# New prices and a shared read resource in the planner that orders a kernel's instructions

## The chip, the core and the metric

The kernel runs on one core of a Trainium2 chip. Five queues run side by side on it: TensorE (PE, whose weight loads are shown as PEld), VectorE (DVE), ScalarE (ACT), GpSimd (POOL) and SyncE (SP, which issues DMAs). Each takes its instructions strictly in the order in which the program holds them; between queues semaphores make an instruction wait for what it needs. The metric is the device time of one execution in microseconds (us), lower is better.

## The reference

One layer of a hybrid encoder over 2048 tokens of 1024 channels. All is float32.

```python
hn = rmsnorm(h, mix_norm_g[i])
proj = hn @ w_in[i]
u, g_ssm, q, k, v, g_attn = jnp.split(proj, SPLITS, axis=-1)
y_ssm = s5_branch(u, ...)                      
y_ssm = y_ssm * jax.nn.silu(g_ssm)
y_att = stick_breaking_branch(q, k, v, q_norm_g[i], k_norm_g[i]) * jax.nn.silu(g_attn)
h = h + jnp.concatenate([y_ssm, y_att], axis=-1) @ w_out[i]
ple_gate = jax.nn.sigmoid(rmsnorm(h, ple_norm_g[i]) @ w_ple_gate[i])
h = h + ple_gate * (p[i] @ w_ple_proj[i])
```

The state-space branch has 32 groups of 16 channels with a 64-wide complex state; each step needs a recurrence over the sequence. The attention branch has 8 heads of 64. For a block of 128 queries it computes, with z the scaled scores, weights exp(log_sigmoid(z) + the sum of log_sigmoid(-z) over all later keys before the query), strictly causal. In the kernel that sum of logarithms is a running product.

## The kernel before

**Stages.** First the input is normalised and transposed, and u is projected (`phase_u`). Then eight batches of four state-space groups run (`ssm_pack`, `ssm_batch`), with the gates of that branch (`gate_unit`) and the first attention projections among them. Attention follows: four head pairs, each over 16 query blocks, skewed by eight blocks against one another; while it runs, the projections of later blocks (`attn_proj`) and the GLU of the state-space branch (`glu_z`, `glu_unit`) are placed among it. Last come the output projection and the per-layer gate for 16 blocks of 128 tokens (`phase_out`). Products in float32 are made from three matmuls of values that are split into a high and a low part (`mm3`, L542 to L544, and `mm3x`, L657 to L659); the split takes one ACT copy (L514 or L492) and one DVE subtraction (L60 or L71).

**State space.** `ssm_pack` makes the matrices of a batch: on DVE the products bn and tm (L60, 128x1024), on POOL the three products at L350 to L352 (stC and tm, 128x1024); PE transposes bn (L358), ACT copies it into stB (L359). `ssm_batch` multiplies (ps_b, L407), rotates on DVE and POOL (rot at L60, swp at L419), scans (L421), goes through a chain of short DVE instructions on 32 columns (b_en, b_ew, the scan b_h at L439, b_H) with swaps of partition halves on ACT (L428, L429), scans again (L450), rotates back (L453 on POOL), and yields. Later PE makes ps_y from it (L467 to L470).

**Attention.** A block of `attn_block` takes its keys in pieces of up to 512. For a piece and each of two heads: PE scores (ps_z, L718, row-tiled), ACT two sigmoids (px at L723, be at L728), POOL a causal mask on the diagonal (two selects, L732), DVE the running product (`tensor_tensor_scan`, L734, which reads px twice), POOL the multiply be by px (L736). Then PE transposes be in 64x64 tiles (ps_wt, L527), ACT or DVE copies it (ws, L745 or L743), and PE multiplies by the values (ps_o, L753, column-tiled). A projection adds 24 matmuls of 512 columns (ps_qk), a root mean square whose power runs on POOL (L508, 128x4), a normalisation on DVE (qn), and transposes (ps_tq). So DVE and POOL both work on data in SBUF during the same microseconds.

**The order.** The program is written in a natural order; `arrange` then fixes the order of every queue. `plan` walks over all instructions, finds what each one must wait for, and prices it with `duration`, which gives two numbers: how long the engine is taken, and how much later the result is there. `list_schedule` plays the program by these prices: the engine that is free first takes the ready instruction of the lowest rank; a change of PE between row-tiled, column-tiled and full matmuls costs 0.2 us and is avoided within 4 us of rank; DMAs share a link. `best_order` plays it forward and backward six times, taking the times of each pass as ranks of the next, and keeps the forward order with the earliest planned end. Only that order reaches the chip: neither a planned time nor a planned wait does. On the chip an instruction starts as soon as it heads its queue and its inputs are there. The lines below are those of before; the change lies behind them, so that L numbers of the stages are the same in both kernels.

Of the kernel before, what the change touches and what calls it, by code (L numbers as in the profile page):

```python
# [1048 lines left out]
def duration(i, name, outs, ins, psum):  # L1049

    n = max([a[1] for a in outs + ins] or [1])
    eng = str(i.engine).split(".")[-1]
    if name == "InstDMACopy":
        return (0.6 if eng == "Pool" else 0.45), 0.0
    if name == "InstMatmult":
        cols, kind = outs[0][1], ins[0][2]
        if i.is_transpose:
            return (0.031 if ins[0][0] <= 64 else 0.109), 0.12
        if "float32r" in kind or "bfloat16" in kind:
            return {512: 0.228, 256: 0.120}.get(cols, max(cols / 2255.0, 0.058)) / (2 if ins[0][0] <= 64 else 1), 0.12  # L1060
        half = min(outs[0][0], ins[0][0]) <= 64
        return (1 if half else 2) * max(cols / 1160.0, 0.056), 0.12
    if eng == "Activation":
        return 0.193 + n * 0.00082, 0.0
    if eng == "Pool":
        if name == "InstTensorTensor" and "pow" in str(i.op).lower():
            return 0.45 + 0.15 * n, 0.0
        base, slope = {"InstMemset": (0.1, 0.0008), "InstTensorCopy": (0.5, 0.001), "InstTensorScalarPtr": (0.3, 0.001), "InstTensorScalarAffineSelect": (0.35, 0.0008)}.get(name, (0.47, 0.00175))
        return base + slope * n, 0.0
    if name == "InstTensorScalarPtr" and i.is_tensor_tensor_scan:  # L1070
        return 0.22 + n * 0.0027, 0.0
    if name in ("InstMemset", "InstTensorCopy") and not psum:
        return 0.11 + n * 0.0006, 0.0
    return 0.15 + n * 0.00107, 0.0


def plan(tc, pools):

    mybir_i = list(tc.nc.cur_bb.bb.instructions)
    first, last = 16512, 229344  # L1080
    open_l, open_r, base, slots, spans, over, home, used = [], [], {}, {}, [], {}, {}, {}
    for p in sorted(pools, key=lambda p: p.id):
        kb = int(p.kb_per_partition_size() * 1024)
        if str(p.space).split(".")[-1] != "SB":
            base[p.id] = 0
        else:
            side = open_r if "right" in str(p.side) else open_l
            born = int(p.alloc_inst.name.split("-")[1])
            while side and side[-1][2] is not None and side[-1][2] < born:
                side.pop()  # L1090
            at = side[-1][0] if side else (last if side is open_r else first)
            lo = at - kb if side is open_r else at
            end = p.release_inst
            side.append((lo if side is open_r else lo + kb, p.id, None if end is None else int(end.name.split("-")[1])))
            base[p.id] = lo
            for q, l2, h2, e2 in spans:
                if l2 < lo + kb and lo < h2 and e2 is not None and int(e2.name.split("-")[1]) < int(p.alloc_inst.name.split("-")[1]):
                    over.setdefault(p.alloc_inst.name, []).append(e2.name)
            spans.append((p.id, lo, lo + kb, end))
        for sp, size, tag, addr, _ in p.gen_slots(0):  # L1100
            home[tag] = p.alloc_inst.name, p.release_inst.name if p.release_inst is not None else None
            slots.setdefault(tag, []).append((str(sp).split(".")[-1], base[p.id] + addr, size // P))
    turn, tiles, held, pre, length, opened, soft, mode = {}, {}, {}, [], [], {}, [], {}
    number = {i.name: k for k, i in enumerate(mybir_i)}
    for k, i in enumerate(mybir_i):
        if type(i).__name__ == "BassTilePoolBoundary":
            pre.append(set())
            soft.append({number[q] for q in over.get(i.name, [])} | used.get(i.name, set()))
            length.append((0.0, 0.0, 0))
            continue  # L1110
        need, ins, outs, loose, psum = set(), [], [], set(), False
        for w, accs in ((0, i.ins), (1, i.outs)):
            for a in accs:
                b = getattr(a, "bass_ap", None)
                if b is None:
                    continue
                t, n = b.tensor, 1
                ap = [(int(s), int(c)) for s, c in b.ap]
                for s, c in a.ap[1:]:
                    n *= int(c)  # L1120
                (outs if w else ins).append((int(a.ap[0][1]), n, str(a.dtype)))
                if type(t).__name__ != "Tile":
                    continue
                shape = tuple(int(x) for x in t.shape)
                if t.name not in tiles:
                    mine = slots[t.tag]
                    q = turn[t.tag] = turn.get(t.tag, -1) + 1
                    sp, lo, size = mine[-q % len(mine)]
                    tiles[t.name] = rec = (sp, [], [], k)
                    if t.tag in opened:  # L1130
                        loose.add(opened[t.tag])
                    opened[t.tag] = k
                    if sp != "DRAM":
                        kept = []
                        for l2, h2, r2 in held.get(sp, []):
                            if l2 < lo + size and lo < h2:
                                need.update(r2[2])
                                if lo <= l2 and h2 <= lo + size:
                                    continue
                            kept.append((l2, h2, r2))  # L1140
                        held[sp] = kept + [(lo, lo + size, rec)]
                sp, accesses, users, born = tiles[t.name]
                loose.add(born)
                a0, r0 = home[t.tag]
                loose.add(number[a0])
                used.setdefault(r0, set()).add(k)
                if sp == "PSUM":
                    psum = True
                    f = (0, P, 1)
                    w = 1  # L1150
                elif sp == "DRAM":
                    row = shape[-1] if len(shape) < 3 else shape[1] * shape[2]
                    o = int(b.offset)
                    reach = o + sum((c - 1) * s for s, c in ap if s > 0)
                    f = (o // row, reach // row + 1, -1)
                else:
                    f = seen_footprint(tuple(ap), int(b.offset), shape)
                kept = []
                for r in accesses:
                    j, wj, g = r  # L1160
                    if j != k and (w or wj) and f[0] < g[1] and g[0] < f[1] and f[2] & g[2]:
                        need.add(j)
                        if w and f[0] <= g[0] and g[1] <= f[1] and (f[2] == -1 or (g[2] != -1 and not g[2] & ~f[2])) and sp != "DRAM":
                            continue
                    kept.append(r)
                accesses[:] = kept + [(k, w, f)]
                users.append(k)
        need.discard(k)
        loose.discard(k)
        pre.append(need)  # L1170
        soft.append(loose - need)
        length.append(duration(i, type(i).__name__, outs, ins, psum) + ((outs[0][0] * outs[0][1] * 4 if type(i).__name__ == "InstDMACopy" else 0),))
        if type(i).__name__ == "InstMatmult":
            mode[k] = "rows" if ins[0][0] <= 64 else "cols" if outs[0][0] <= 64 else "all"
    return mybir_i, pre, soft, length, mode


_seen = {}
# [9 lines left out]
def list_schedule(ops, pre, soft, length, mode, rank, near=4.0, change=0.2):  # L1188

    import heapq  # L1190
    n = len(ops)
    eng = [f"none{k}" if type(i).__name__ == "BassTilePoolBoundary" else str(i.engine) for k, i in enumerate(ops)]
    after, open_, free, wait, ready, order, now = [[] for _ in ops], [len(p) + len(q) for p, q in zip(pre, soft)], {}, {}, {}, {}, {}
    start, done, link = [0.0] * n, [0.0] * n, 0.0
    for k in range(n):
        for q in (*pre[k], *soft[k]):
# [16 lines left out]
    for _ in range(n):  # L1213
        best = None
        for e in free:
            while wait[e] and wait[e][0][0] <= free[e]:
                _, r, k = heapq.heappop(wait[e])
# [9 lines left out]
        t, late, e = best  # L1227
        if late:
            k = heapq.heappop(wait[e])[2]
        else:  # L1230
            m = min((h for h in ready[e] if ready[e][h]), key=lambda h: ready[e][h][0][0] - near * (h == now[e]))
            k = heapq.heappop(ready[e][m])[1]
        t = max(t, due(k))
        if now[e] != mode.get(k):
            t += change
            now[e] = mode.get(k)
        start[k] = t
        free[e] = t + length[k][0]
        if length[k][2]:
# [89 lines left out]
```

## Time and profile before

| | us |
|---|---|
| runs, three | 1605.84, 1606.33, 1608.09 |
| median | 1606.33 |
| span of the profiled execution, from its first to its last instruction | 1604.8 |
| mean granted TensorE clock over the span | 0.986 |
| instructions | 31108 |

The profiled execution has no time of its own but its span. A group of the profile reads: line, engine, operation, tile written <- tiles read, shapes, count | busy time in us, mean ns of one | idle time of the engine before them and who ended it. A row of waits reads: who waited <- for whom: us in total, times, longest. A row of the timeline reads: start, duration, engine, line, operation, tiles. The row of a stretch gives for each engine its busy time and, in brackets, its instructions, then the clock that the TensorE throttle granted (1 is full), the share of the DMA engines and GB/s. A matmul's duration holds its way through the array, so that neighbours overlap.

### The profile page before, as it was taken

How to read it: one execution, taken by the hardware profiler on the slowest of the kernel's cores; microseconds unless marked ns; L12 is line 12 of the kernel's file. 1: busy time of each engine (PE TensorE's matmuls, PEld its weight loads, DVE VectorE, ACT ScalarE, POOL GpSimd, SP SyncE). 2: the span in 40 equal slices, each digit the busy share in tenths (PEclk: the TensorE clock that was granted, in tenths of full speed). 3: DMA queues.
4: the chain of work that ended last, by engine and by line, in shares of the span. 5: the costliest groups of instructions: out<-in, count | busy, mean ns of one | idle time of the engine just before them, and what ended most of it. 6: DMA issues, size and time to landing. Idle time of an engine off the chain costs nothing.

```text
span 1604.8 us, 31108 instructions
## 1 busy us (share of the span) xinstructions
PE 1548.5 (96%) x11878; PEld 1254.5 (78%) x11878; DVE 1079.1 (67%) x1980; ACT 825.2 (51%) x1850; POOL 766.3 (48%) x882
## 2 busy tenths in 40 slices
PE   6999898999999999999999999999989999999998
PEld 6998888987777777777777776777678788888887
DVE  6895948868678997789987899748764432332322
ACT  6643435456566776677766777646544221121211
POOL 2242434437578898688967798747630000000000
PEclk9999999999999999999999999999999999999999
DMA  9897535455332323323233234432354221212210
GB/s 294 262 289 194 175 118 181 156 174 193 113 113 84 112 91 132 113 85 108 95 132 112 86 109 112 109 96 68 107 164 126 83 79 50 86 60 69 64 49 33
DMA packets 147670, 195.58 MB, mean 122 GB/s; under 512 B 63697, under 2 KB 110753, under 8 KB 136129
## 3 DMA queue, kind: packets, MB, share of 16 engines
q1 hardware_dynamic: 145552, 186.45, 36.1%
q0 software_dynamic: 1968, 7.15, 2.2%
q8 instruction: 94, 1.54, 0.4%
q14 instruction: 56, 0.45, 0.1%
HBM read 145.44 MB, written 48.12 MB: 121 GB/s over the span
## 4 chain that ended last, share of the span: by engine, by line
PE 79%; DVE 11%; issue 4%; POOL 3%; ACT 1%; DMA 1%; SPq 0%; POOLq 0%; DVEq 0%; ACTq 0%
PE ps_qk L657 7%; PE ps_qk L659 7%; PE ps_qk L658 7%; PE ps_o L753 6%; PE ps_z L718 5%; PE ps_wt L527 4%; PE ps_g L659 4%; PE ps_h L657 4%; PE ps_h L658 4%; PE ps_g L658 4%; PE ps_h L659 4%; PE ps_g L657 4%; DVE px L734 3%; POOL be L736 2%; PE ps_u L543 2%
## 5 line engine op out<-in xcount | busy, mean ns | idle before, releaser
L736 POOL TENSOR_TENSOR be<-be,px 128x512 f32<-128x512 f32 (+3 forms) x320 | 404.1, 1275 | 136.6 <-DVE px L734 51.0
L734 DVE TENSOR_TENSOR_SCAN px<-px 128x512 f32<-128x512 f32 (+3 forms) x320 | 424.6, 1338 | 52.6 <-ACT px L723 37.0
L723 ACT ACTIVATE px<-ps_z 128x512 f32<-128x512 f32 (+3 forms) x320 | 170.0, 539 | 78.8 <-PE ps_z L718 51.9
L657 PE MATMUL ps_qk<-w_w,xt 128*128 128x512 f32 x480 | 198.7, 414 | 1.2 <-DVE gn L60 1.2
L658 PE MATMUL ps_qk<-w_w,xt 128*128 128x512 f32 x480 | 195.4, 407 | 0.0
L659 PE MATMUL ps_qk<-w_w,xt 128*128 128x512 f32 x480 | 195.3, 407 | 0.0
L508 POOL TENSOR_TENSOR rs_h<-rs_h,mhalf 128x1 f32<-128x1 f32 x16 | 9.1, 572 | 381.8 <-DVE rs_h L67 381.8
L728 ACT ACTIVATE be<-ps_z 128x512 f32<-128x512 f32 (+3 forms) x320 | 170.4, 545 | 5.4 <-PE ps_wt L527 5.4
L745 ACT ACTIVATE ws<-ps_wt 128x512 f32<-128x512 f32 (+3 forms) x256 | 129.0, 540 | 79.3 <-PE ps_wt L527 78.5
L718 PE MATMUL ps_z<-k,q 64*128 64x512 f32 (+3 forms) x960 | 138.5, 392 | 2.4 <-ACT be L728 1.5
L753 PE MATMUL ps_o<-ws,v 128*64 128x128 f32 x2176 | 138.3, 278 | 0.0
L753 PEld LDWEIGHTS ps_o<-ws,v 128*64 128x64 f32 x2176 | 118.7, 138 | 22.2 <-issue 18.1
L527 PEld LDWEIGHTS ps_wt<-ident,be 64*128 64x128 f32 x2176 | 83.1, 138 | 51.6 <-issue 25.6
L657 PEld LDWEIGHTS ps_qk<-w_w,xt 128*128 128x128 f32 x480 | 90.2, 188 | 32.1 <-issue 11.9
L659 PEld LDWEIGHTS ps_qk<-w_w,xt 128*128 128x128 f32 x480 | 90.3, 188 | 24.2 <-issue 5.7
L658 PEld LDWEIGHTS ps_qk<-w_w,xt 128*128 128x128 f32 x480 | 90.5, 189 | 23.5 <-issue 5.8
L527 PE MATMUL ps_wt<-ident,be 64*128 64x64 f32 x2176 | 102.9, 229 | 5.8 <-POOL be L736 2.8
L514 ACT ACTIVATE yr<-yt 128x512 fp32r<-128x512 f32 x32 | 20.2, 632 | 162.7 <-PE ps_h L659 157.3
L657 PE MATMUL ps_h<-w_w,yr 128*128 128x512 f32 x256 | 100.7, 393 | 2.3 <-ACT yr L514 2.3
L659 PE MATMUL ps_g<-w_wg,hr 128*128 128x512 f32 x256 | 101.5, 397 | 0.0
L658 PE MATMUL ps_g<-w_wg,hr 128*128 128x512 f32 x256 | 101.1, 395 | 0.0
L658 PE MATMUL ps_h<-w_w,yr 128*128 128x512 f32 x256 | 100.6, 393 | 0.0
(378 smaller groups left out, 3608.5 us busy)
## 6 DMA issues: line engine op xcount, KB each, us to landing
xt<-hn SPq DMA_DIRECT2D x60, 1024.0 KB, 4.9
hn<-xt SPq DMA_DIRECT2D x16, 1024.0 KB, 9.5
wst<-in_w_in_dram SPq DMA_DIRECT2D x48, 256.0 KB, 5.3
xg<-hn SPq DMA_DIRECT2D x12, 1024.0 KB, 7.0
x<-in_x_dram SPq DMA_DIRECT2D x16, 512.0 KB, 7.0
out_dram<-o SPq DMA_DIRECT2D x32, 256.0 KB, 2.0
h<-in_x_dram SPq DMA_DIRECT2D x15, 512.0 KB, 4.3
u<-uq POOLq DMA_DIRECT2D x4, 1024.0 KB, 18.3
```

The costliest lines, as they stand in the source:

```text
L527: e.nc.tensor.transpose(ps[h][:, 64 * k:64 * k + 64], v[r], e.ident[r, r])
L543: mm(out, wh, xl, start=False, stop=False)
L657: mm(out, xh, wh, start=first, stop=False)
L658: mm(out, xh, wl, start=False, stop=False)
L659: mm(out, xl, wh, start=False, stop=last)
L718: nc.tensor.matmul(z[:, :n], q[half[h], a], A.k[ch][half[h], b, :n], start=s == 0, stop=s == 2)
L723: nc.scalar.activation(px[:, :n], z[:, :n], AF.Sigmoid, scale=-(HD ** -0.5))
L728: nc.scalar.activation(be[:, :n], z[:, :n], AF.Sigmoid, scale=HD ** -0.5)
L734: nc.vector.tensor_tensor_scan(rv, rv, rv, initial=1.0 if carry[h] is None else carry[h], op0=ALU.mult, op1=ALU.bypass)
L736: nc.gpsimd.tensor_tensor(be[:, :n], be[:, :n], px[:, 1:n + 1], op=ALU.mult)
L745: nc.scalar.activation(dst, ps, AF.Copy)
L753: nc.tensor.matmul(po[half[h], :P], A.v[sb][:, h], w[:, h, b], start=sb == i, stop=sb == 0)
```

## The change

All of it is in the planner. `duration` gets other numbers: most engine times are shorter, and most instructions get a delay of 0.03 to 0.11 us between the end of the engine time and the result, where it was 0 before (0.12 on PE). `plan` counts for each instruction the tiles in SBUF that it reads with more than one element to a partition, and `shares` marks instructions from that: on POOL any that reads one, on DVE any that reads two, and a copy or an operation with a scalar that reads one and touches no PSUM. In `list_schedule` marked instructions of the two engines exclude each other: `port` holds the time at which the last marked one ends, and the next starts no earlier.

```diff
@@ duration
         if i.is_transpose:
-            return (0.031 if ins[0][0] <= 64 else 0.109), 0.12
+            return (0.031 if ins[0][0] <= 64 else 0.109), 0.11
         if "float32r" in kind or "bfloat16" in kind:
-            return {512: 0.228, 256: 0.120}.get(cols, max(cols / 2255.0, 0.058)) / (2 if ins[0][0] <= 64 else 1), 0.12
+            return max(cols / 2400.0 + 0.0136, 0.107) / (2 if ins[0][0] <= 64 else 1), 0.11
...
     if eng == "Activation":
-        return 0.193 + n * 0.00082, 0.0
+        return (0.05 if psum else 0.094) + n * 0.00083, 0.065 if psum else 0.03
     if eng == "Pool":
         if name == "InstTensorTensor" and "pow" in str(i.op).lower():
-            return 0.45 + 0.15 * n, 0.0
-        base, slope = {"InstMemset": (0.1, 0.0008), "InstTensorCopy": (0.5, 0.001), "InstTensorScalarPtr": (0.3, 0.001), "InstTensorScalarAffineSelect": (0.35, 0.0008)}.get(name, (0.47, 0.00175))
-        return base + slope * n, 0.0
+            return 0.35 + 0.15 * n, 0.08
+        base, slope = {"InstMemset": (0.04, 0.0008), "InstTensorCopy": (0.4, 0.001), "InstTensorScalarPtr": (0.25, 0.001), "InstTensorScalarAffineSelect": (0.14, 0.0008)}.get(name, (0.12, 0.00186))
+        return base + slope * n, 0.09
     if name == "InstTensorScalarPtr" and i.is_tensor_tensor_scan:
-        return 0.22 + n * 0.0027, 0.0
-    if name in ("InstMemset", "InstTensorCopy") and not psum:
-        return 0.11 + n * 0.0006, 0.0
-    return 0.15 + n * 0.00107, 0.0
+        return 0.05 + n * 0.0022, 0.03
+    if name in ("InstMemset", "InstTensorCopy", "InstTensorScalarPtr") and not psum and not i_tt(i):
+        return 0.07 + n * 0.0006, 0.03
+    return 0.07 + n * 0.00104, 0.03
+
+def i_tt(i):
+    return getattr(i, "is_scalar_tensor_tensor", False)
@@ plan
+                read += not w and n > 1 and type(t).__name__ == "Tile" and slots_space(slots, t.tag) == "SB"
...
-        length.append(duration(...) + ((... DMA bytes or 0),))
+        length.append(duration(...) + ((... DMA bytes or 0), shares(i, type(i).__name__, read, psum)))
+
+def slots_space(slots, tag):
+    return slots[tag][0][0]
+
+def shares(i, name, read, psum):
+    eng = str(i.engine).split(".")[-1]
+    if eng == "Pool":
+        return read > 0 and name != "InstDMACopy"
+    return eng == "DVE" and (read > 1 or (read == 1 and not psum and name in ("InstTensorCopy", "InstTensorScalarPtr")))
@@ list_schedule
-    ..., now = ..., {}
+    ..., now, port = ..., {}, 0.0
...
         if now[e] != mode.get(k):
             t += change
             now[e] = mode.get(k)
+        if length[k][3]:
+            t = max(t, port)
+            port = t + length[k][0]
         start[k] = t
         free[e] = t + length[k][0]
```

Shapes, tiles, buffers, matmuls, DMAs and their number are those of before.

More of the change, by code (lines that the diff above doesn't have):

```diff
@@ L1108, in plan @@
             soft.append({number[q] for q in over.get(i.name, [])} | used.get(i.name, set()))
-            length.append((0.0, 0.0, 0))
+            length.append((0.0, 0.0, 0, False))
             continue
-        need, ins, outs, loose, psum = set(), [], [], set(), False
+        need, ins, outs, loose, psum, read = set(), [], [], set(), False, 0
         for w, accs in ((0, i.ins), (1, i.outs)):
@@ L1171, in plan @@
         soft.append(loose - need)
-        length.append(duration(i, type(i).__name__, outs, ins, psum) + ((outs[0][0] * outs[0][1] * 4 if type(i).__name__ == "InstDMACopy" else 0),))
+        length.append(duration(i, type(i).__name__, outs, ins, psum) + ((outs[0][0] * outs[0][1] * 4 if type(i).__name__ == "InstDMACopy" else 0), shares(i, type(i).__name__, read, psum)))
         if type(i).__name__ == "InstMatmult":
@@ L1192, in list_schedule @@
     eng = [f"none{k}" if type(i).__name__ == "BassTilePoolBoundary" else str(i.engine) for k, i in enumerate(ops)]
-    after, open_, free, wait, ready, order, now = [[] for _ in ops], [len(p) + len(q) for p, q in zip(pre, soft)], {}, {}, {}, {}, {}
+    after, open_, free, wait, ready, order, now, port = [[] for _ in ops], [len(p) + len(q) for p, q in zip(pre, soft)], {}, {}, {}, {}, {}, 0.0
     start, done, link = [0.0] * n, [0.0] * n, 0.0
```

## The prediction

> **What bounds the kernel now.** The change alters no instruction, only the order in which each engine's queue holds them, so the first question is what an order can win. I read the page's busy shares and its chain of waits.
>
> ```profile
> PE 1548.5 (96%) x11878; PEld 1254.5 (78%) x11878; DVE 1079.1 (67%) x1980; ACT 825.2 (51%) x1850; POOL 766.3 (48%) x882
> PE 79%; DVE 11%; issue 4%; POOL 3%; ACT 1%; DMA 1%; SPq 0%; POOLq 0%; DVEq 0%; ACTq 0%
> ```
>
> PE is busy for 1548.5 of 1604.8 us, and the chain that ends last runs through PE for 79% and through DVE for 11%. An order can win back at most the 56 us in which PE idles, the time it loses at a lower clock, and what it spends on changing the kind of matmul. Next, the stretches: projection of u and state-space part (0 to 330), attention (330 to 1185), output (1185 on). Columns: PE, weight loads, DVE, ACT, POOL busy, clock, DMA.
>
> ```profile
> 0.00:330.00 330.00, 297.19 (x2428) 287.10 (x2429) 248.76 (x599) 163.84 (x337) 116.82 (x81) 0.95 0.67 206
> 330.00:1185.00 855.00, 838.01 (x7412) 631.94 (x7411) 688.09 (x1154) 568.45 (x1351) 640.34 (x785) 0.99 0.35 113
> 1185.00:1605.00 420.00, 413.26 (x2042) 335.41 (x2040) 142.22 (x229) 92.87 (x163) 9.14 (x16) 1.00 0.24 73
> ```
>
> Of the idle PE time, 33 us lie in the first stretch, 17 in attention, 7 in the output. The output stretch is PE at full clock with everything else light, so no order changes it by much. The first stretch is where PE waits and where its clock falls (0.95). Then the waits of PE, and PE's sequencer where it waits for nothing shown ("issue"), which is what a change from row-tiled (L718, L527) to full (L657) or column-tiled (L753) matmuls looks like:
>
> ```profile
> PE ps_qk L657 <- DVE b_en L60: 4.9, 1, 4.9
> PE ps_b L407 <- ACT stB L359: 4.6, 1, 4.6
> PE ps_g L543 <- DVE zr L60: 3.7, 3, 3.0
> ...
> PE ps_y L470 <- DVE rot L60: 2.8, 3, 2.0
> PE ps_wt L527 <- POOL be L736: 2.8, 4, 1.7
> ```
>
> ```profile
> PEld ps_wt L527 <- issue: 25.6, 86, 0.4
> ...
> PEld ps_o L753 <- issue: 18.1, 53, 0.5
> PEld ps_qk L657 <- issue: 17.0, 39, 5.1
> ...
> PEld ps_z L718 <- issue: 14.8, 49, 0.4
> ```
>
> **What the change reprices.** The old prices are near what an instruction took in the crowd, the new ones near what it takes alone, with the crowd put in as a resource that one engine holds. The trace lets both be tested. Alone or nearly so, a 512-wide scan took 1.28 us and a 512-wide POOL multiply 1.09; in attention's middle their means are 1553 and 1431 ns.
>
> ```profile
> 498.24 1.09 POOL L736 TENSOR_TENSOR be<-be,px 128x512 f32<-128x512 f32 x1
> 499.43 1.01 POOL L508 TENSOR_TENSOR rs_qk<-rs_qk,mhalf 128x4 f32<-128x4 f32 x1
> 500.01 1.28 DVE L734 TENSOR_TENSOR_SCAN px<-px 128x512 f32<-128x512 f32 x1
> 500.40 0.97 POOL L732 TENSOR_SCALAR_AFFINE_SELECT px<-px 128x128 f32<-128x128 f32 x1
> ```
>
> Below are the groups of 500 to 1000 us: mean ns of one behind the comma.
>
> ```profile
> L734 DVE TENSOR_TENSOR_SCAN px<-px 128x512 f32<-128x512 f32 x152 | 234.9, 1553 | 15.8 <-ACT px L723 11.9 <-POOL px L732 3.6
> L60 DVE TENSOR_TENSOR qn<-qn,rs_qk 128x256 f32<-128x256 f32 x40 | 28.3, 707 | 14.0 <-POOL rs_qk L508 9.3 <-POOL px L725 4.5
> ...
> L71 DVE SCALAR_TENSOR_TENSOR w_w<-wst,gmix,w_w 128x512 fp32r<-128x512 f32 x12 | 11.2, 939 | 0.0
> ```
>
> ```profile
> L736 POOL TENSOR_TENSOR be<-be,px 128x512 f32<-128x512 f32 x152 | 215.8, 1431 | 59.1 <-DVE px L734 24.5 <-DVE px L727 8.7 <-ACT be L728 6.3
> L732 POOL TENSOR_SCALAR_AFFINE_SELECT be<-be 128x128 f32<-128x128 f32 x83 | 57.4, 693 | 3.3 <-ACT be L728 3.1
> L732 POOL TENSOR_SCALAR_AFFINE_SELECT px<-px 128x128 f32<-128x128 f32 x83 | 38.7, 470 | 8.4 <-ACT px L723 8.0 <-PE ps_qk L659 0.3
> L508 POOL TENSOR_TENSOR rs_qk<-rs_qk,mhalf 128x4 f32<-128x4 f32 x40 | 48.0, 1200 | 7.2 <-DVE rs_qk L67 6.1 <-DVE v L674 0.2
> ```
>
> Old price of the scan: 0.22 + 512 x 0.0027 = 1.60 us; new: 0.05 + 512 x 0.0022 = 1.18 plus 0.03. Multiply: 0.47 + 512 x 0.00175 = 1.37 old; 0.12 + 512 x 0.00186 = 1.07 plus 0.09 new. So the new lengths fit the lone instruction, and the lock that stands for the crowd is real: the select at 500.40 took 0.97 us against a mean of 0.47 and came free as the scan of 500.01 ended. One thing is priced wrongly: the power (L508) is made to hold the resource for 0.35 + 4 x 0.15 = 0.95 us, but the scan of 500.01 began 0.58 us into the power of 499.43 and took its 1.28 regardless.
>
> How tight is that resource in the plan? In 500 to 1000 there are 215 scans and 215 multiplies:
>
> ```profile
> 500.00:1000.00 500.00, 287.93 (x215) 1.00 0.32 106
> ```
>
> ```profile
> 500.00:1000.00 500.00, 272.38 (x215) 1.00 0.32 106
> ```
>
> By the new prices: 152 x 1.176 + 152 x 1.072 = 341.7; the 63 smaller of each at their middle width (256: 0.613 and 0.596) 76; 166 selects x 0.242 = 40; 40 powers x 0.95 = 38. Together 496 us of 500, before smaller holders on DVE: 40 normalisations qn at 0.07 + 256 x 0.00104 = 0.34 and 12 weight splits at 0.60, 21 us. About 517: more than the stretch has, though the chip did it in 500; without the powers' 38 us it is 479.
>
> [...]
>
> **The sum, part by part.** Nothing is removed or added on the chip; the terms are the stretches, each with what a new order can do to it.
>
> First stretch. Three PE waits there are made by the lock that the old planner did not know:
>
> ```profile
> 196.50 2.89 DVE L71 SCALAR_TENSOR_TENSOR w_w<-wst,gmix,w_w 128x512 fp32r<-128x512 f32 x1
> ...
> 199.91 1.91 DVE L60 TENSOR_TENSOR rot<-rot,swp 128x512 f32<-128x512 f32 x1
> ```
>
> ```profile
> 195.57 3.27 POOL L352 TENSOR_TENSOR stC<-stC,tm 128x1024 f32<-128x1024 f32 x1
> 198.92 2.35 POOL L351 TENSOR_TENSOR tm<-pwi,ct 128x1024 f32<-128x1024 f32 x1
> ```
>
> ```profile
> 266.76 1.85 DVE L60 TENSOR_TENSOR b_en<-swp,tabs 128x32 f32<-128x32 f32 x1
> ...
> 269.13 1.92 DVE L60 TENSOR_TENSOR b_ew<-b_ew,tabs 128x32 f32<-128x32 f32 x1
> ...
> 271.32 1.93 DVE L439 TENSOR_TENSOR_SCAN b_h<-b_d,b_en 128x32 f32<-128x32 f32 x1
> ```
>
> ```profile
> 268.64 2.37 POOL L352 TENSOR_TENSOR stC<-stC,tm 128x1024 f32<-128x1024 f32 x1
> 271.09 2.08 POOL L351 TENSOR_TENSOR tm<-pwi,ct 128x1024 f32<-128x1024 f32 x1
> ```
>
> ```profile
> 198.00:210.00 12.00, 7.08 (x24) 5.62 (x23) 10.40 (x20) 4.27 (x10) 4.16 (x3) 0.72 0.25 87
> 270.00:286.00 16.00, 11.40 (x60) 11.21 (x60) 15.41 (x23) 6.82 (x14) 6.28 (x4) 0.68 0.46 171
> ```
>
> At 196.50 a weight split of DVE sits behind POOL's product stC for 2.89 us and the rotation after it behind POOL's tm; what follows on DVE's queue is late, and PE's first ps_qk waits 4.9 us. At 266 to 273 three DVE instructions on 32 columns take 1.9 us each, one behind each POOL product; ACT's swaps queue behind them, and with them the stB copy for which ps_b waits 4.6 us. With ps_y's 2.8 that is 12.3 us of PE idleness, and right behind it the clock is low: 0.72 over 12 us and 0.68 over 16, that is 3.4 + 5.1 = 8.5 us. All of it is 21 us. The new planner sees these products as 2.0 us each in which DVE's two-input work stands still, and can put other matmuls (ps_sg, ps_qk) ahead of those that must wait. It cannot make POOL start later than its inputs allow, and the chain scan, swap, product, scan keeps its length. Bounds: a gain of 21, and below nothing a loss of 12, if as many new waits appear elsewhere. I take half of the gain, **-10 us**: the waits are few, one place each, and the cover (some matmul that is ready) was running right up to each.
>
> Attention. PE is busy 838 of 855 us, so of waits at most 17 us can go; the four issue rows sum to 75.5 us in 227 places; without the longest, 5.1 us, which is the wait for b_en seen from the weight loads, 70 us in 226, 0.31 us each (an upper bound, as the previous matmul is still draining in part of it). A tenth fewer of them is -7 us. On the other side the plan is paced by a resource of 517 in 500, 3.4% of 855 us = 29 us if the chip followed that pace. I take **0**: prices nearer to the chip and a falsely priced power pull against each other.
>
> End of attention and output. The split of zr is priced at 0.60 us plus 0.03, old 0.70, and took more than twice that:
>
> ```profile
> L60 DVE TENSOR_TENSOR zr<-zt,zr 128x512 fp32r<-128x512 f32 x16 | 23.7, 1492 | 1.2 <-ACT zr L514 1.2
> 1135.00:1186.00 51.00, 42.64 (x327) 32.47 (x325) 36.22 (x45) 25.93 (x47) 28.60 (x26) 0.87 0.44 142
> ```
>
> so the wait of ps_g on it (3.7 us in all) and the dip of the clock behind it (0.13 x 51 = 6.6 us) are no better planned than before: **0**, from -8 to +8. Output: **0**.
>
> Sum: 1604.8 - 10 = 1594.8 us of span; the median of the runs lies 1.5 us over the profiled span, so 1596.3, rounded to **1596**.
>
> **The rivals.**
> A. *The plan is paced by the resource, and PE pays* (slower). The planner believes DVE and POOL can't keep up with PE in attention's middle. A planned PE that runs out of ready work takes whatever comes ready next, so the emitted PE order alternates more often between L718/L527 and L657/L753. The price is 0.31 us a change at most; with a quarter more than the 226, 57 x 0.31 = 18 us, from the point where these outweigh the 10 us of the first stretch, some 30 further changes. With half of the 29 us as waits of ps_wt for be besides: 1606 + 18 + 14 = 1638 at its worst, 1620 as a middle. For it: 517 in 500. Against it: the old plan was crowded too (a DVE full of 1.60 us scans) and its order is good.
> B. *The order changes and the gain doesn't come* (within 0.2%, which is 3.2 us and about what these runs can tell from no change). POOL starts whatever has its inputs, so the same collisions come back at other places: 1606. [...]
> C. *More than hoped*: all 21 us of the first stretch, and a tenth of the issue time in attention: 1606 - 21 - 7 = 1578. For it: the old lengths are too long wherever an instruction runs alone (1.60 against 1.28 us), so the old plan kept work back without need. Against it: part of the chain in the first stretch is latency that no order shortens.
>
> **How the numbers follow.** Forecast (1584 to 1603) 0.42; C (below 1584) 0.10; B 0.08; A 0.40, of which 0.08 lie above 1638. Hence faster 0.52, same 0.08, slower 0.40. Signs are nearly even, so the range reaches from C's middle to A's worst, 1575 to 1638; the forecast's own range is 1584 to 1603.
>
> **What would show it.** Right: ps_qk waits for b_en and ps_b for stB no longer or half as long, the clock of the state-space stretch rises from 0.95, attention starts some 10 us earlier, and the issue rows keep their 226 places and 70 us within a tenth. The scan's and the multiply's means should stay within a tenth of 1553 and 1431, since the lock is not avoided, only planned for. Wrong, for A: issue rows well above 226 places, or ps_wt waiting for be in many places instead of 4, and an attention stretch longer than 855 us. Wrong, for B: as many microseconds of PE waits in the first stretch, at other lines. A plan that puts PE-only work of the output stretch into attention isn't possible, since its weights take the place of attention's tiles.

## The result, and the profile after

The changed kernel takes 1620.3 us (median of 4 runs, 1618.9 to 1623.4), the kernel before 1607.2 beside it: a ratio of 1.0086, 95% interval 1.0073 to 1.0098. It is slower, by 13 us. The profiled spans, 1604.8 and 1621.6 us, differ by 17. Here is the busy line of the changed kernel's page, with the chain of waits and two groups.

```profile
PE 1557.0 (96%) x11878; PEld 1260.4 (78%) x11878; DVE 1036.1 (64%) x1980; ACT 818.0 (50%) x1850; POOL 725.8 (45%) x882
...
PE 83%; DVE 6%; ACT 3%; issue 3%; DMA 2%; POOL 2%; POOLq 0%; DVEq 0%; ACTq 0%; SPq 0%
...
L736 POOL TENSOR_TENSOR be<-be,px 128x512 f32<-128x512 f32 (+3 forms) x320 | 398.7, 1261 | 181.0 <-DVE px L734 106.7
L734 DVE TENSOR_TENSOR_SCAN px<-px 128x512 f32<-128x512 f32 (+3 forms) x320 | 407.4, 1290 | 43.1 <-ACT px L723 22.1
```

DVE is busy 43 us less (1079.1 before) and POOL 40 less (766.3) on the same instructions, so a bit less time is spent with one of the two held up by the other, which the prediction calls the lock: in before the 196 scans of 512 columns with a multiply or a select of POOL beside them take 1.42 us in the median and the other 28 take 1.28; the 157 multiplies of 512 columns with a scan beside them take 1.88 and the other 67 take 1.09. With the change 182 scans and 143 multiplies have such company. It doesn't help. POOL's multiplies now stand 106.7 us waiting for a scan, where it was 51.0. PE, with the same 11878 matmuls, is busy longer and idle longer.

Where the time went shows best by milestones of the work itself. All kernels here run the same 320 multiplies of L736; counted from zero, the start of the 40th, 80th, 240th and last (319th) are read from the timeline of POOL. The last column is from there to the end of the span.

| kernel | 40th starts at | 40th to 80th | 80th to 240th | 240th to last | rest | span |
|---|---|---|---|---|---|---|
| before | 460.2 | 94.9 | 377.8 | 245.2 | 426.7 | 1604.8 |
| after | 457.6 | 97.1 | 395.1 | 242.8 | 429.0 | 1621.6 |
| difference | -2.6 | +2.2 | **+17.3** | -2.4 | +2.3 | +16.8 |

All of the loss lies in the middle of attention. The same stretches as windows (PE, weight loads, DVE, ACT, POOL busy, clock, DMA), first before, then after:

```profile
555.00:933.00 378.00, 376.32 (x3528) 280.87 (x3529) 318.08 (x560) 263.69 (x654) 304.96 (x386) 1.00 0.31 106
```

```profile
554.70:949.80 395.10, 387.95 (x3540) 287.65 (x3539) 313.94 (x563) 262.35 (x658) 283.41 (x385) 0.99 0.31 104
```

The counts are nearly the same, but POOL's milestones do not bound PE's work exactly: after has 15 matmuls of ps_qk more in its stretch than before (784 against 769), at 0.235 us from one start to the next some 3.5 of the 17.3 us. PE idled 1.7 us and now idles 7.2; its busy time grew by 12 us, of which the same 3.5 are those matmuls. The profile's own caution applies: a matmul's end is modelled, so short pauses between matmuls count as busy. They can be counted from the starts: neighbouring matmuls start more than 0.35 us apart in 10 places before (5.4 us in all) and in 36 after (21.8 us). POOL is busy for 22 us less in a stretch that is 17 us longer. Neither engine is short of time; work comes to them late. In these two windows POOL waited for scans (total, times, longest):

```profile
POOL be L736 <- DVE px L734: 23.8, 22, 1.7
```

```profile
POOL be L736 <- DVE px L734: 59.1, 42, 3.1
```

In the first stretch the waits that the prediction named shrank, and others grew. These are PE's waits with the change in 100 to 330 us, where before stood b_en (4.9), stB (4.6) and rot (2.8):

```profile
PE ps_b L407 <- DMA us<-u: 4.3, 1, 4.3
PE ps_y L470 <- DVE rot L60: 1.6, 2, 1.0
PE ps_sg L542 <- DVE sg L60: 1.5, 2, 0.9
PE ps_b L407 <- ACT stB L359: 0.3, 1, 0.3
```

With the few smaller ones, all waits of PE in 100 to 330 fell from 17.0 to 7.9 us, and the clock over 0 to 330 us rose from 0.95 to 0.98. In 0 to 100 us they were 15.9 before, 13.0 of them for x, of which 11.2 the start of the kernel:

```profile
PE ps_x L527 <- ACT x L561: 13.0, 2, 11.2
```

With the change they are 21.5, and the start of the kernel is the 7.3 of ps_prep:

```profile
PE ps_x L527 <- ACT x L561: 9.0, 3, 4.1
PE ps_prep L201 <- DMA nre<-in_ssm_a_re_dram: 7.3, 1, 7.3
PE ps_x L527 <- DVE xt L60: 3.9, 3, 3.3
```

The longest wait for x is an effect of the new order on POOL's queue. From the timeline of POOL and of PE:

```profile
81.57 2.82 POOL L592 DMA_DIRECT2D u<-uq  x1 [5.65 <-ACT xt L514]
84.41 2.47 POOL L350 TENSOR_TENSOR stC<-pwr,cts 128x1024 f32<-128x1024 f32 x1
86.85 2.02 POOL L351 TENSOR_TENSOR tm<-pwi,ct 128x1024 f32<-128x1024 f32 x1
88.84 2.01 POOL L350 TENSOR_TENSOR stC<-pwr,cts 128x1024 f32<-128x1024 f32 x1
90.81 0.56 POOL L508 TENSOR_TENSOR rs_x<-rs_x,mhalf 128x1 f32<-128x1 f32 x1
```

```profile
92.61 1.12 PE L527 MATMUL ps_x<-ident,x 64*128 64x64 f32 x16 [4.08 <-ACT x L561]
```

POOL's products of the state-space batches have moved ahead, in among the last normalisations of x. A DMA issue on POOL that takes 2.82 us (the planner prices it at 0.6 in both versions) and three products stand in front of a power that PE needs, and PE stands for 4.1 us. Attention's first ps_z starts earlier, at 336.1 instead of 345.0, but by the 40th multiply only 2.6 us are left of that.

Last, the changes between kinds of matmul, which the slower rival had blamed:

```profile
PEld ps_wt L527 <- issue: 24.1, 77, 0.6
...
PEld ps_z L718 <- issue: 15.5, 49, 0.4
...
PEld ps_o L753 <- issue: 13.6, 42, 0.4
...
PEld ps_qk L657 <- issue: 9.4, 34, 0.4
```

202 places and 62.6 us, against 226 and 70 before: fewer, not more. In the middle of attention, where the loss lies, these four rows have 114 places and 35.0 us, against 117 and 36.4: no difference worth naming.

### The profile page after: what moved, and what is told of

It is laid out like the page before. It is cut to its first block, busy times and chain, and to the rows that moved or that the text cites. A ratio compares the mean times of both kernels' runs of the same rounds, so it can differ in the third digit from the quotient of the medians.

```text
span 1621.6 us, 31159 instructions
## 1 busy us (share of the span) xinstructions
PE 1557.0 (96%) x11878; PEld 1260.4 (78%) x11878; DVE 1036.1 (64%) x1980; ACT 818.0 (50%) x1850; POOL 725.8 (45%) x882
## 3 DMA queue, kind: packets, MB, share of 16 engines
q8 instruction: 94, 1.54, 0.4%
## 4 chain that ended last, share of the span: by engine, by line
PE 83%; DVE 6%; ACT 3%; issue 3%; DMA 2%; POOL 2%; POOLq 0%; DVEq 0%; ACTq 0%; SPq 0%
PE ps_qk L657 8%; PE ps_o L753 8%; PE ps_qk L658 8%; PE ps_qk L659 7%; PE ps_z L718 6%; PE ps_wt L527 5%; PE ps_g L659 4%; PE ps_g L657 4%; PE ps_g L658 4%; PE ps_h L657 4%; PE ps_h L658 4%; PE ps_h L659 4%; PE ps_tq L690 1%; PE ps_sg L542 1%; PE ps_sg L543 1%
## 5 line engine op out<-in xcount | busy, mean ns | idle before, releaser
L736 POOL TENSOR_TENSOR be<-be,px 128x512 f32<-128x512 f32 (+3 forms) x320 | 398.7, 1261 | 181.0 <-DVE px L734 106.7
L734 DVE TENSOR_TENSOR_SCAN px<-px 128x512 f32<-128x512 f32 (+3 forms) x320 | 407.4, 1290 | 43.1 <-ACT px L723 22.1
L728 ACT ACTIVATE be<-ps_z 128x512 f32<-128x512 f32 (+3 forms) x320 | 170.8, 557 | 13.7 <-PE ps_wt L527 13.6
L718 PE MATMUL ps_z<-k,q 64*128 64x512 f32 (+3 forms) x960 | 150.2, 400 | 14.3 <-ACT be L728 13.2
L753 PE MATMUL ps_o<-ws,v 128*64 128x128 f32 x2176 | 141.7, 281 | 4.5 <-DVE yat L60 3.9
L753 PEld LDWEIGHTS ps_o<-ws,v 128*64 128x64 f32 x2176 | 120.1, 139 | 26.1 <-issue 13.6
L527 PEld LDWEIGHTS ps_wt<-ident,be 64*128 64x128 f32 x2176 | 86.8, 141 | 50.2 <-issue 24.1
L718 PEld LDWEIGHTS ps_z<-k,q 64*128 64x128 f32 x960 | 82.5, 190 | 45.1 <-ACT be L728 21.6
L657 PE MATMUL ps_h<-w_w,yr 128*128 128x512 f32 x256 | 100.7, 394 | 1.5 <-DVE h L60 1.5
```

The source lines that it names most:

```text
L527: e.nc.tensor.transpose(ps[h][:, 64 * k:64 * k + 64], v[r], e.ident[r, r])
L657: mm(out, xh, wh, start=first, stop=False)
L718: nc.tensor.matmul(z[:, :n], q[half[h], a], A.k[ch][half[h], b, :n], start=s == 0, stop=s == 2)
L728: nc.scalar.activation(be[:, :n], z[:, :n], AF.Sigmoid, scale=HD ** -0.5)
L734: nc.vector.tensor_tensor_scan(rv, rv, rv, initial=1.0 if carry[h] is None else carry[h], op0=ALU.mult, op1=ALU.bypass)
L736: nc.gpsimd.tensor_tensor(be[:, :n], be[:, :n], px[:, 1:n + 1], op=ALU.mult)
```

## The experiments

Each ran beside the kernel before; ratios are against that. The theories: P, the resource is overbooked in the plan and paces attention; S, the short lengths leave PE no slack; C, any new order loses against one to which the kernel's sizes were fitted. Later theories are D and L, which the expectations explain where they come up.

**1. The parts of the change, one by one.** New lengths without the resource (`lengths_only`):

```diff
-        if length[k][3]:
+        if False:
             t = max(t, port)
```

> The new lengths without the shared resource. Theory P (the resource is overbooked in the plan, and PE's order is paced by it; it cost attention 20 us): attention goes back to some 837 us, and the total to 1597 to 1610, the upper end if the gain of the first stretch needs the resource. Theory S (the shorter lengths leave PE no slack, so it stands before results that aren't there): 1618 or more, with the waits of ps_z and ps_wt at least those of the changed kernel. Theory C (any new order loses against one that the sizes were fitted to): 1612 to 1625.

Measured: 1677.3 us, ratio 1.0441 (1.0425 to 1.0457). P alone is refuted by this. S is met in the total and in the waits of ps_wt, but not in those of ps_z (3.7 us for be, against 13.2 in the changed kernel). The 80th multiply starts at 581.2 instead of 555.1, and 80th to 240th takes 411. The waits of PE, whole kernel:

```profile
PE ps_tq L690 <- DVE qn L60: 15.0, 7, 3.4
PE ps_tq L691 <- DVE gn L60: 9.3, 8, 2.7
PE ps_wt L527 <- DVE ws L743: 8.7, 10, 2.4
...
PE ps_wt L527 <- POOL be L736: 5.7, 9, 1.8
```

PE now stands before results of DVE and POOL, which such a plan prices as if each ran alone: 1.18 us for a scan of 512 columns, whose mean is 1.54 in before.

The resource with the old lengths (`port_only`): `duration` is that of before, `shares` and `port` are in.

> The resource with the old lengths. In 500 to 1000 us it is then booked 152 x 1.602 + 152 x 1.366 + 63 x 0.91 + 63 x 0.92 + 166 x 0.452 + 40 x 1.05 = 684 us of 500. Theory P: attention is paced still more, 1650 to 1900. Theory S: the old lengths give the slack back, 1600 to 1612. Theory C: 1612 to 1625.

Measured: 1784.5 us, ratio 1.1117 (1.1100 to 1.1133). P's case, and the opposite of S's: 80th to 240th takes 488.5 us. With lengths that already contained the crowd (1.60 us for a scan that takes 1.28 alone), the lock is counted twice, and the chip stays behind what it could have done. It doesn't follow the plan's pace to the letter: by the 684 us booked in 500 the middle would be a good third longer than 378, some 517 us. PE's largest wait is of another kind than above, for a bank of scores that ACT has not yet emptied:

```profile
PE ps_z L718 <- ACT be L728: 50.7, 59, 3.3
```

So each half of the change by itself is far worse than both together: the old lengths had been the planner's substitute for the lock.

Which lengths stood in? New ones for PE and ACT alone (`pe_act_new`), DVE and POOL as before, nothing shared:

```diff
-        return 0.193 + n * 0.00082, 0.0
+        return (0.05 if psum else 0.094) + n * 0.00083, 0.065 if psum else 0.03
```

(with the numbers of PE's matmuls likewise)

> The kernel before with the new lengths of PE and ACT alone; DVE and POOL keep the old ones, and nothing is shared. With all new lengths and nothing shared it was 1677. Theory D (the old DVE and POOL lengths stood in for the lock, and taking them away without the resource made those 71 us): 1595 to 1620. Theory A (ACT's shorter lengths leave PE no slack): 1640 or more, with PE waiting for ACT's ws and be.

Measured: 1597.1 us, ratio 0.9941 (0.9922 to 0.9961), its seven runs from 1592 to 1604. D is borne out: the 71 us of `lengths_only` don't come without DVE's and POOL's new lengths. ACT's shorter ones do no harm in the total; the middle takes 382.1 us here, in the slowest of the seven runs.

**2. The power that holds the resource.** Nowhere (`no_pow`):

```diff
-        return read > 0 and name != "InstDMACopy"
+        return read > 0 and name != "InstDMACopy" and not (name == "InstTensorTensor" and "pow" in str(i.op).lower())
```

> The change, but the power of L508 does not hold the resource, as in the trace. It books 64 x 0.95 = 61 us less over the kernel, 38 in 500 to 1000. Theory P: a good part of the 20 us that attention lost comes back, 1602 to 1612. Theory S: nothing comes back, 1617 to 1623. Theory C: anywhere from 1612 to 1625, no relation to the 61 us.

Measured: 1623.4 us, ratio 1.0111 (1.0094 to 1.0128), the profiled span 1616.8: by the total that is S, and P's 1602 to 1612 is missed. By the milestones, P where it applies: 80th to 240th fell from 395.1 to 380.6 us, but the 40th starts at 467.2 instead of 457.6, since the order of the first stretch became a new one too. So the edit was confined to attention (`np_late`):

```diff
-        length.append(duration(i, ...) + (..., shares(i, type(i).__name__, read, psum)))
+        length.append(duration(i, ...) + (..., shares(i, type(i).__name__, read, psum) and not (k >= ATT[0] and "pow" in str(getattr(i, "op", "")).lower())))
```

(ATT[0] is the number of the first instruction of attention's loop.)

> The change, but from attention's loop on the power does not hold the resource; before it the change as it was. Measured by where POOL's multiplies start: the 80th to the 240th took 378 us before, 395 with the change, 381 where no power held the resource at all, but that kernel was 10 us later at the 40th. Theory P (the falsely booked power paces attention): 381 to 384 in the middle and the 40th at 456 to 460, total 1604 to 1611. Theory C (any new order costs about as much, wherever it is new): the middle anywhere from 380 to 400, total 1612 to 1625.

Measured: 1611.2 us, ratio 1.0025 (1.0013 to 1.0037); the 40th at 457.7, the middle 382.4. That is P in the milestones, and P's upper end (1611) in the total. The middle of `np_late` and that of `no_pow` hold the same numbers of matmuls of each kind but for one, so they are hardly two independent orders. And the suspected cost doubled (`pow_double`):

```diff
-            port = t + length[k][0]
+            port = t + length[k][0] * (2 if "pow" in str(getattr(ops[k], "op", "")).lower() else 1)
```

> The change, but a power holds the resource for twice its length (its own length as before). 40 powers of 500 to 1000 us book another 38 us. Theory P: the middle (80th to 240th multiply) goes from 395 us to 410 to 430, the total to 1635 to 1665. Theory C: 1612 to 1630, middle 385 to 400.

Measured: 1653.0 us, ratio 1.0290 (1.0273 to 1.0306), the middle 406.3. P has the total right and the middle too long (410 to 430). Three booked lengths of an instruction that the edits leave as it is, and three paces. PE's work in the three stretches differs a little: with 766, 784 and 747 matmuls of ps_qk, the step from `np_late` to after is some 4 us smaller than the milestones say, and the step to `pow_double` some 9 us larger. POOL's rows of L736 in the middle, for `np_late`, after and `pow_double` (length of the stretch, busy, count):

```profile
554.30:936.70 382.40, 197.53 (x161) 0.99 0.31 104
```

```profile
554.70:949.80 395.10, 192.34 (x160) 0.99 0.31 104
```

```profile
559.30:965.60 406.30, 195.84 (x161) 0.98 0.29 98
```

POOL works 192 to 198 us on the same multiplies in 382, 395 and 406 us. What grows is its waiting for scans, in `np_late` and in `pow_double`:

```profile
POOL be L736 <- DVE px L734: 44.6, 33, 2.3
```

```profile
POOL be L736 <- DVE px L734: 76.5, 46, 5.1
```

44.6, 59.1, 76.5 us for a power that books nothing, its length, and twice that. Waits for scans alone don't set the pace, though: `np_late` has 21 us more of them than before and a middle only 4.6 us longer.

How a booking that the chip never sees makes a scan late shows on DVE's queue. From the timelines of ACT, DVE and POOL in the changed kernel:

```profile
974.43 0.62 ACT L723 ACTIVATE px<-ps_z 128x512 f32<-128x512 f32 x1
974.41 1.22 DVE L734 TENSOR_TENSOR_SCAN px<-px 128x512 f32<-128x512 f32 x1
977.16 0.29 DVE L60 TENSOR_TENSOR q<-ps_tq,q 128x128 fp32r<-128x128 f32 x1 [1.53 <-ACT q L514]
977.37 0.14 DVE L727 COPY px<-px 128x1 f32<-128x1 f32 x1
977.43 2.39 DVE L734 TENSOR_TENSOR_SCAN px<-px 128x512 f32<-128x512 f32 x2
978.78 1.92 POOL L736 TENSOR_TENSOR be<-be,px 128x512 f32<-128x512 f32 x1 [1.72 <-DVE px L734]
```

DVE is free at 975.63. The last px that ACT wrote is there at 975.05, and POOL has done its last work on a px at 975.76. Yet DVE stands idle to 977.16, since the split of q heads its queue and waits for ACT; the scan comes behind it, and POOL waits 1.72 us for the scan. The split reads one tile in SBUF and one in PSUM, so it doesn't hold the resource in the plan. DVE's waits for it in the middle, for before, `np_late`, after and `pow_double`:

```profile
DVE q L60 <- ACT q L514: 4.6, 8, 0.9
```

```profile
DVE q L60 <- ACT q L514: 3.9, 4, 1.4
```

```profile
DVE q L60 <- ACT q L514: 15.7, 15, 2.2
```

```profile
DVE q L60 <- ACT q L514: 30.2, 21, 4.8
```

The waits of DVE's copy ws for PE, which doesn't hold the resource either, go the same way: 5.4, 9.6, 17.5 and 22.1 us. So the more the plan books, the more often instructions that book no resource stand on DVE's queue ahead of scans, and the chip keeps that order, as in the 1.53 us before 977.16. That the plan puts them there because its scans stand back is argued, since no run shows a planned time. Nor was a booking of the same size taken from instructions that do hold the lock, so it is open whether the booking costs because it is false or because it is too much.

**3. Where the new prices are good.** For everything that the program holds before attention's loop (`new_early`):

```diff
-        length.append(duration(i, ...) + (..., shares(...)))
+        new = (k < ATT[0]) == True
+        length.append((duration if new else duration_old)(i, ...) + (..., new and shares(...)))
```

> New lengths and resource for all instructions that the program holds before attention's loop, old lengths and no resource from it on. Theory P: the first stretch keeps its 9 us and attention doesn't lose, 1594 to 1602. Theory S: as P, since the short lengths matter in attention alone. Theory C: a new order again, 1607 to 1625.

Measured: 1603.7 us, ratio 0.9986 (0.9977 to 0.9995), between the 1594 to 1602 of P and the 1607 and more of C. The middle takes 377.8, exactly as before, but the 40th starts at 462.2, 2 us later than before. Attention's first ps_z came 8 us sooner and nothing was won by it. For the state-space batches alone, with the projection of u at the old prices (`new_ssm`): the same with `SSM0[0] <= k < ATT[0]`, where SSM0[0] is the first instruction of the batches' loop.

> New lengths and resource for the state-space batches alone, with the projection of u before them and attention after them at the old lengths without resource. With the change PE's waits in 100 to 330 us fell from 17.0 to 7.9 us and those of 0 to 100 us rose from 15.9 to 21.5. Theory L (the lock's waits of the state-space stretch are what the new planner saves; the projection of u is where it pays them back): the 40th multiply starts at 449 to 457 instead of 460, total 1594 to 1603. Against it (the stretch is bound by its chain, and what is saved there is waited for at attention's start, as where new prices held for everything before attention: the 40th at 462): 1603 to 1609.

Measured: 1594.1 us, ratio 0.9918 (0.9903 to 0.9934); the 40th at 446.6 instead of 460.2, everything behind it as before (94.9, 377.8, 244.4, 426.3). That is L, with the 40th even earlier than its 449 to 457: in these two orders, repricing the projection of u as well costs 15.6 us at the 40th multiply. How much of the 13.6 us is due to the resource is another matter, to which the next experiment speaks.

**4. How much an order scatters.** The kernel before, with one number of the planner moved by 5% (`change021`; `change019` has 0.19):

```diff
-def list_schedule(ops, pre, soft, length, mode, rank, near=4.0, change=0.2):
+def list_schedule(ops, pre, soft, length, mode, rank, near=4.0, change=0.21):
```

> The kernel before, with the planner's cost of a change between kinds of matmul at 0.21 us in place of 0.20: an order that is new for no reason. Theory P: within 0.5% of before, 1598 to 1614. Theory C: slower as the change is, 1612 to 1625.

> The kernel before with that cost at 0.19 us. One more order that is new for no reason; no theory says its sign. If orders scatter by about 1%, 1590 to 1625 with the middle of attention at 375 to 385 us; if the 0.21 was worth something by itself, 1606 or slower.

Measured: 1591.7 us, ratio 0.9906 (0.9890 to 0.9922), and 1584.0 us, ratio 0.9853 (0.9836 to 0.9869). Both lie below everything that the theories allowed. Both ways is faster, so neither number is better in itself: the order of before is an unlucky one among its neighbours. That holds for the first stretch above all: the 40th multiply starts at 455.2 and 448.5 us, against 460.2, with a clock of 0.98 over the first 330 us and without PE's waits for b_en and for stB before ps_b, though neither plan knows of the resource. The same waits are gone in `pe_act_new` (452.7). So of the 13.6 us of `new_ssm` (446.6) up to 11.7 can come with another order alone. All waits of PE in 100 to 330 us are 13.6, 12.3 and 12.3 us in these three, against 17.0 before, 10.0 in `new_ssm` and 7.9 after. The changed kernel, moved in the same way (`after_change021`):

> The change, with the planner's cost of a change between kinds of matmul at 0.21 us in place of 0.20. The kernel before became 1.0% faster by this alone. Theory P (the booked power paces the middle of attention, whatever the order elsewhere): the 80th to the 240th multiply again 390 to 400 us, the total anywhere in 1607 to 1630. Theory C (what the change lost is the luck of one order): the middle 375 to 385, total 1590 to 1612.

Measured: 1630.0 us, ratio 1.0145 (1.0130 to 1.0160), with the middle at 393.1, as P said. C is refuted for the middle: the change keeps its 393 to 395 us under another order, and the old prices keep their 373 to 378 under three. Two orders of the change lie at 1620 and 1630, three of the old prices at 1584, 1592 and 1607. The one pair that was compared understates what the change costs, if anything.

**5. A version that beats both** (`ssm_021`): `new_ssm` with 0.21.

> New lengths and resource for the state-space batches alone (1594.1) and the cost of a change at 0.21 us (1591.7 for the kernel before). If what each won is its own and they add: 1577 to 1584. If they are two draws of an order: 1585 to 1605.

Measured: 1582.2 us, ratio 0.9845 (0.9830 to 0.9859). That lies in the range given for gains that add, but they add only in part: up to the 40th multiply it is as good as `new_ssm` (446.1), behind it as good as `change021` (middle 378.1, rest 420.7), and the 5.0 us that `change021` won before the 40th don't come on top.

## Why the prediction was wrong

**The step that failed** is attention's term, taken as 0 because "prices nearer to the chip and a falsely priced power pull against each other". They don't: nearer prices won nothing there. With the power's booking gone the middle takes 381 to 382 us, with the old prices 378. So the booking of the power was left to act, and it cost 13 to 15 of the 17 us by the milestones, and by the ratios of `np_late` and the change (1.0025 and 1.0086) 10 of 14 us over the whole kernel. (The milestones take in the additional matmuls of ps_qk; without them it is 9 to 10 of 14 in the middle too.) Why 3 to 5 us are left there when the power books nothing stays open; `pe_act_new`, with the old prices of DVE and POOL, also takes 382. The size seemed within reach: 517 us booked in 500, 479 without the power, is a pace 3.4% too slow, 13 us on the 378 of the middle. But that fit is partly luck. By the same count the doubled booking, 555 us in 500, should cost 42 us, and cost 28.5. PE's share there (376.3 of 378.0 us busy) had already said that prices could win little and that a plan could lose much; the best order here, `change019`, has the middle at 373.0.

**The first stretch** (-10 us) came to -2.6 at the 40th multiply. The signs that were named came: the waits for b_en, stB and rot went or shrank, the waits of 100 to 330 us fell by 9.1, the clock rose from 0.95 to 0.98, and attention's first ps_z came 8.9 us earlier. `new_ssm` even has 13.6 us at the 40th. But that the resource in the plan is what does it isn't shown, since `change021`, `change019` and `pe_act_new` lose the waits for b_en and stB without it and win 5.0, 11.7 and 7.5 us there. What the term left out is that the same prices also reorder the projection of u, where waits rose by 5.6 us. The lower bound named that ("as many new waits appear elsewhere"); the term itself did not weigh it.

**End of attention and output** (0, and 0): -2.4 and +2.3 us, near 0 as said.

**The rivals.** A gave the sign, the place and, with 1620 as its middle, the total. Its way was wrong: changes between kinds of matmul became fewer, and ps_wt does not wait for be in many places (0.7 us once). The pace reaches PE through short pauses, 36 in place of 10 in the middle; the waits of ps_z for banks (13.2 us in all, 1.5 before) lie before and behind the middle but for 1.4 us. B's remark held beside this: the lock was not avoided, as the means of 512 columns in 500 to 1000 us, 1553 and 1431 ns for scan and multiply, are 1555 and 1397 with the change. C's 1578 is near what the best version reaches, by other means.

**The evidence that was weighed too lightly** was 517 us in 500, worked out and then set against a mere tendency. The chance of 0.40 for "slower" should have been the larger one. The range, 1575 to 1638, held the time, but it was wide enough for either sign. (Its lower end was called C's middle, which is 1578.)

**On the booking of the power.** The change lets the power wait until the resource is free and then keep it for its whole length. The trace of before bears out the first half and not the second. A power that starts while a scan runs is still there 0.80 us after the scan's end (0.80 to 0.83 us in all 12 such places of before), and a scan that starts while a power runs takes its usual time, 1.22 us here:

```profile
608.98 1.27 DVE L734 TENSOR_TENSOR_SCAN px<-px 128x512 f32<-128x512 f32 x1
609.04 2.01 POOL L508 TENSOR_TENSOR rs_qk<-rs_qk,mhalf 128x4 f32<-128x4 f32 x1
...
670.12 1.01 POOL L508 TENSOR_TENSOR rs_qk<-rs_qk,mhalf 128x4 f32<-128x4 f32 x1
670.24 1.22 DVE L734 TENSOR_TENSOR_SCAN px<-px 128x512 f32<-128x512 f32 x1
```

The runs above put a price on the booking as a whole, 13 to 15 us by the milestones: `no_pow` and `np_late` drop both halves of it, and a plan in which the power waits and then doesn't hold was not run.

## What to carry to other kernels

A planner's prices that were fitted in the crowd contain the crowd: replacing them by lone lengths and modelling the crowd must be done together, and each booked hold must be shown in the trace, for a hold that isn't there, as that of the power here, shapes the plan, and the chip keeps the plan's order. Before repricing, look stage by stage at what is left to win; where the bounding engine is already busy for 99.6%, a truer price has little to win and much to lose. And measure the scatter of orders first, by moving a number that should not matter: here it was 16 to 23 us, more than the change under study.

## What the runs showed of the hardware

Behind PE's longer waits in before its granted clock is low for some microseconds: 0.72 over 12 us from 198, 0.68 over 16 us from 270, as the prediction's windows show. No run here separates the pause from what follows it, but orders differ in their clock. The mean granted clock of before, after, `change021` and `ssm_021`:

```profile
core 0: 1604.8 us, clock 0.986
```

```profile
core 0: 1621.6 us, clock 0.983
```

```profile
core 0: 1589.5 us, clock 0.993
```

```profile
core 0: 1579.8 us, clock 0.993
```

As an estimate, 1 minus the clock, times the span, before lost 22 us and `change021` 11: of the 15 us between their spans, up to 11 are clock. The same count gives 5 of the 17 us between before and after. The clock also moves from run to run of one order: the seven runs of `pe_act_new` go from 1592.5 us at 0.996 to 1604.3 at 0.986. The other surprise was priced by experiment 2: of POOL's instructions on SBUF not all hold the lock for their length. In before 16 scans of 512 columns start while a power on 128x4 runs and no multiply or select of POOL is under way; they take 1.28 us in the median, as those with no multiply or select beside them do, and 1.39 at most, with up to 0.90 us of the power to come. The other way round, 12 powers start during a scan and take 1.61 us in the median, up to 2.01; the median of the other 52 is 1.01.
